# Two blocks on one core: where additions stand in VectorE's order, and what GpSimd adds for norms and gating

## The chip, the cores and the metric

The kernel runs on one core of one Trainium2 chip. The metric is the device time of one execution in microseconds (us), as the median of three runs. A core has a matrix engine (TensorE, PE in profile rows, with its weight loads as PEld), VectorE (DVE), ScalarE (ACT), GpSimd (POOL) and SyncE (SP). Each engine works through a queue of its own in order and waits on semaphores for what other engines or DMAs have to finish first. TensorE writes to PSUM; GpSimd works on SBUF.

## The reference, cut to what matters

One sequence of 512 tokens of width 1024 goes through a first block of two layers and a second block of two. All arithmetic is float32. What the change touches:

```python
def rms_norm(x, g):                       # before every mixer and every feed-forward half: 8 times
    y = x * rsqrt(mean(x * x, axis=-1) + EPS);  return y * g

def moe_swiglu(x, ...):                   # first block, second layer: 8 experts, 2 per token
    logits = x @ w_router + b_router;  top_logit, top_e = top_k(logits, 2);  top_w = softmax(top_logit)
    for e in range(8):                    # rows of the tokens that chose e
        h = silu(xb @ w_gate[e]) * (xb @ w_up[e]);  y[tokens] += (h @ w_down[e]) * w
    return y

def spatial_gating(u, v, v_g, w_s, b_s):  # second block, both layers: 4 heads of 64 channels
    v = rms_norm(v) * v_g
    # per head h, within each window of 128 tokens, with w_s masked to a causal pattern of blocks:
    # out[t, h, :] = u[t, h, :] * (sum over s in the window of w_s[h, t, s] * v[s, h, :]  +  b_s[h, t])
```

## The kernel before, in words

**Data.** The running activation lies transposed in eight tiles `s.xT[k]` of 128 channels x 512 tokens. Weights stream from DRAM in tiles of 128x1024 (`load`, L130). Each is split into a high half, a rounding to the matrix engine's faster float format by ScalarE (`hi`, L97), and a low half, the rest, by VectorE (`lo`, L113) or GpSimd (L111). A product then takes three matmuls: high x high, high x low, low x high (L138 to L140, in the experts L1067 to L1069). A raw tile has 8 buffers in the layer with the experts, the halves 5; so the splitting runs a few tiles ahead of TensorE and no more.

**Order.** A planner sets each engine's queue before the program runs. It goes by the order in the source, by modelled durations and by what it takes to be ready, and lets an instruction of lower rank run early where it takes its inputs to be there. `after(s, ins)` (L629) fixes one thing: what stands in its block is queued behind `ins` on that engine.

**Norms.** `norm_tile(k)` (L209) splits tile k and squares it (L219 ScalarE, L221 GpSimd). GpSimd adds squares 1 to 5 to square 0 in `sqa` (L225); squares 6 and 7 stay apart. `norm_end` (L227) sums the three tiles over channels with matmuls against a constant (L233), in the order `sqa`, 6, 7: four matmuls of 128x2 per tile, which the trace shows as eight records.

**Experts** (`moe`, L975). Behind the router eight 128x512 tiles of normalized tokens are made by transposes (L1044, in PSUM tags `sc` and `tp`, two banks each) and split. A branch (L1160) covers the case of overfull experts, which is not taken with these inputs. Experts 0 and 1 get their rows by a matmul with a one-hot matrix (L1170); the others gather theirs from `xn`, a copy in DRAM. For this copy GpSimd adds the high and low halves of the eight tiles (L1195) and stores them (L1196); its queue also holds the scatters into a small table (L1188) and the loads of it (L1199, L1201). Each expert is `up` (24 weight tiles in three column groups c of 8) and `down` (11 tiles f); a second group of tokens, 32 per expert, is multiplied from the raw tiles in float32 on a quarter of the columns (`others`, L1077). In experts 0 and 7 all low halves are VectorE's (`les` is "v").

Experts 0 to 6 scatter results to `ys` in DRAM. Expert 7 keeps its own in SBUF (`keep`), and meanwhile the rows of `ys` are loaded into pairs of tiles, `early`, by 16 loads on GpSimd's queue (L1252). `mid`, called behind each down tile f, adds each pair at f = 2 (L1300) and at f = 6 transposes the sums back (`sums`, L1144, one PSUM bank `st`) and adds them to `xT` (L254). A last stage multiplies expert 7's kept rows by one-hot matrices (L1314), adds them to `xT` and starts the next norm.

**Gating** (`gmlp`, L1722). For each of four heads: four float32 matmuls, one per 128 tokens, into PSUM partitions 0 to 63 (L1744, two records each), one more that adds the bias as a product with a row of ones (L1745), and a VectorE multiplication with 64 rows of `u` (L1748). The bias row is loaded into a rotating tile by ScalarE's queue (L1718). The result is split and used by `out_proj` at the layer's end. The state-space branch, run beside it, has a matmul group (L1626) that alternates between PSUM partitions 0 to 63 and 64 to 127.

Of the kernel before, what the change touches and what calls it, by code (L numbers as in the profile page):

```python
# [46 lines left out]
class Ctx:  # L47
# [58 lines left out]
    def lo(s, out, x, h, scale=None, eng="v"):  # L106
        nc = s.nc
        if scale is not None:
            nc.vector.scalar_tensor_tensor(out, x, scale, h.bitcast(F32), ALU.mult, ALU.subtract)  # L109
        elif eng == "p":  # L110
            nc.gpsimd.tensor_sub(out, x, h.bitcast(F32))  # L111
        else:
            nc.vector.tensor_sub(out, x, h.bitcast(F32))  # L113

    def split(s, x, h, l, scale=None, he="a", le="v"):
        s.hi(h, x, scale, he)
# [92 lines left out]
    def norm_tile(s, k):  # L209
        nc = s.nc  # L210
        g = s.gain[:, k:k + 1]
        h = s.xp.tile([128, S], F32R, name="xh", tag="xh")
        l = s.xp.tile([128, S], F32R, name="xl", tag="xl")
        s.split(s.xT[k], h, l, scale=g)
        s.xh.append(h)
        s.xl.append(l)
        t = s.sqa if k == 0 else s.sqtile()
        if k in s.SQ_ACT:
            nc.scalar.activation(t, s.xT[k], AF.Square)  # L219
        else:  # L220
            nc.gpsimd.tensor_mul(t, s.xT[k], s.xT[k])  # L221
        if k == 0 or k >= KT - 2:
            s.sqs = [t] if k == 0 else s.sqs + [t]
        else:
            nc.gpsimd.tensor_add(s.sqa, s.sqa, t)  # L225
# [749 lines left out]
def moe(s):  # L975
# [63 lines left out]
    xt = [None] * (2 * NT)  # L1039
    for hf in range(2):  # L1040
        for i in range(NT):
            ps = s.P(("sc", "tp")[i % 2])
            for k in range(4):
                nc.tensor.transpose(ps[:, k * 128:k * 128 + 128], s.xT[4 * hf + k][:, i * 128:i * 128 + 128], s.ident)  # L1044
            h = s.xp.tile([128, 512], F32R, name="xth", tag="xh")
            l = s.xp.tile([128, 512], F32R, name="xtl", tag="xl")
            s.hi(h, ps, s.rt[:, i:i + 1])
            with after(s, chosen):
                s.lo(l, ps, h, s.rt[:, i:i + 1])
            xt[2 * i + hf] = (h, l)  # L1050
# [12 lines left out]
    def load3(src, le):  # L1063
        return (*s.load(src, le=le), s.raw)
# [12 lines left out]
                    last = nc.tensor.matmul(out(j), lhs(k), rhs(raw, j), start=k == 0, stop=k == K - 1)  # L1077
        held.clear()

    def up(gu, X, first=(), les=MO_UP):  # L1080

        H, HO = [], s.A((128, FE * 32), F32)
        hold = 2 if s.more is None else HOLD
        for c, (f0, nb) in enumerate(FBLK):
            n = nb * 128
            pp, po, held = [s.P("mm"), s.P("sc")], s.P("o"), []
            for k in range(KT):
                i = KT * c + k
                wh, wl, raw = first.pop(0) if first else load3(gu(i)[:, :2 * n], les[i % len(les)])
                for x in range(2):  # L1090
                    o = slice(x * n, x * n + n)
                    mm3m(pp[x][:, :n], X[1 + k // 2][:, k % 2 * 256:k % 2 * 256 + 128], X[1 + k // 2][:, k % 2 * 256 + 128:k % 2 * 256 + 256],
                         wh[:, o], wl[:, o], k == 0, k == KT - 1)
                held.append((k, raw[:, :2 * n].rearrange("p (x j c) -> p x j c", x=2, j=nb)))
                if len(held) == hold or k == KT - 1:
                    others(held, nb, KT, lambda k: X[0][:, (CAP - 128) * k:(CAP - 128) * (k + 1)], lambda r, j: r[:, :, j],
                           lambda j: po[32 * j:32 * j + 32, 0:256].rearrange("p (x c) -> p x c", x=2))
            g, h = s.T(), s.T()
            nc.scalar.activation(g[:, :n], pp[0][:, :n], AF.Silu)
            nc.vector.tensor_mul(h[:, :n], pp[1][:, :n], g[:, :n])  # L1100
            r = slice(0, 32 * nb)
            go, ho = s.T((128, 128)), s.T((128, 128))
            nc.scalar.activation(go[r], po[r, 0:128], AF.Silu)
            nc.vector.tensor_mul(ho[r], po[r, 128:256], go[r])
            hh, hl = s.A(), s.A()
            with s.late(L_TP):
                ps = s.P("tp")
                for j in range(nb):
                    nc.tensor.transpose(ps[:, j * 128:j * 128 + 128], h[:, j * 128:j * 128 + 128], s.ident)
                s.split(ps[:, :n], hh[:, :n], hl[:, :n])  # L1110
                ps = s.P("tp")
                nc.tensor.transpose(ps[:, r], ho[r], s.ident[r, r])
                nc.scalar.activation(HO[:, 32 * f0:32 * f0 + 32 * nb], ps[:, r], AF.Copy)
            H.append((hh, hl))
        return H, HO

# [71 lines left out]
            nc.gpsimd.indirect_dma_start(out=s.tab[:, :], out_offset=bass.IndirectOffsetOnAxis(ap=place[:, k, i:i + 1], axis=0),  # L1188
                                         in_=m["info"][:, k, i], in_offset=None)

    for hf in range(2):
        for i in range(NT):
            h, l = xt[2 * i + hf]
            t = s.A((128, 512), F32)
            nc.gpsimd.tensor_add(t, h.bitcast(F32), l.bitcast(F32))  # L1195
            nc.gpsimd.dma_start(s.xn[hf * S + i * 128:hf * S + i * 128 + 128, :], t)  # L1196
    at = lambda r: bass.AP(tensor=s.tab.tensor, offset=s.tab.offset + 4 * r, ap=[[4, 32 if r else 128], [4 * CAP, NE], [1, 4]])
    kM, kO = (s.small((128, NE, 4), tag="k" + n, bufs=1) for n in "MO")
    nc.gpsimd.dma_start(kM, at(0))  # L1199
# [56 lines left out]
    for e in range(NE):  # L1256
        if e % 2 and e + 1 < NE:
            G = gather(e + 1)
        H = up(lambda i, e=e: a["moe_gu"][e * KT * len(FBLK) + i], X[e % 2], ahead, "v" if e in (0, NE - 1) else MO_UP)

        def put(x, ps, e=e):
            yt = s.T()
# [32 lines left out]
        s.split(ps, *(v[:, :n] for v in Y[x]), scale=wt[:, NE - 1, w:w + 1])  # L1295

    def mid(f):
        if f == 2:
            for y in chain(*early):
                nc.vector.tensor_add(y[0], y[0], y[1])  # L1300
        if f != 6:
            return
        for k, ps in sums(lambda hf, i: early[hf][i][0], "st"):
            s.residual(k, ps)
# [402 lines left out]
def gmlp_tables(s, L):  # L1707

    nc, a, mixp = s.nc, s.a, s.mixp
    vg = mixp.tile([128, 256], F32, name="vgain")  # L1710
    src = a["gmlp_vg"]
    nc.scalar.dma_start(vg, bass.AP(tensor=src.tensor, offset=src.offset + L * 256, ap=[[0, 128], [1, 256]]))
    wm = s.ldm("c_wmask", (128, 128))
    w = s.A((128, 4, 128), F32)
    nc.scalar.dma_start(w, a["gmlp_wT"][L])
    nc.gpsimd.tensor_mul(w, w, wm.unsqueeze(1).to_broadcast([128, 4, 128]))
    bs = s.T((1, 4, 128))
    nc.scalar.dma_start(bs, a["gmlp_bs"][L:L + 1])  # L1718
    return vg, w, bs


def gmlp(s, L, tabs, vps, u):  # L1722
# [15 lines left out]
        nc.vector.scalar_tensor_tensor(vn.rearrange("p h d -> p (h d)"), vps[c], y[:, c:c + 1], vg, ALU.mult, ALU.mult)  # L1738
        V.append(vn)
    yield 4  # L1740
    for h in range(4):
        ps = s.P(TG["gm"])
        for n in range(NT):
            nc.tensor.matmul(ps[0:64, n * 128:n * 128 + 128], V[n][:, h], w[:, h], start=n == 0, stop=False)  # L1744
        nc.tensor.matmul(ps[0:64], s.ones1[:, 0:64], bs[:, h:h + 1, :].to_broadcast([1, 4, 128]), start=False, stop=True)  # L1745
        t = u[h // 2]
        r = slice(64 * (h % 2), 64 * (h % 2) + 64)
        nc.vector.tensor_mul(t[r], ps[0:64], t[r])  # L1748
        if h % 2 == 1:
            s.dbg("d_sgu%d_%d" % (L, h // 2), t)  # L1750
            mix_tile(s, 2 + h // 2, t)
    yield 4


# [546 lines left out]
```

## Time and profile before

| | |
|---|---|
| median of 3 runs | 2829.59 us (2823.96 to 2833.44) |
| the profiled execution's own time | 2834.34 us |
| its span, first to last instruction | 2832.6 us |
| mean granted TensorE clock | 0.969 of full |
| busy: PE, DVE, ACT, POOL | 96%, 60%, 43%, 25% of the span |
| instructions | 39198 |
| moved by DMA | 354.42 MB, mean 125 GB/s |

The busy share of TensorE counts matmuls that overlap with the next one, so 96% is the share of the span in which at least one is under way. A row of a timeline has the start in us, the duration in us, the engine, the source line, the operation with the names of the tiles written and read, and, in brackets, the time for which the engine stood idle before it and what ended that. Neighbours of the same kind are merged (x8), with one start and one duration for all. In a list of waits the numbers are the total, the count and the longest.

### The profile page before, as it was taken

The page shows a single profiled execution, that of the slowest core. Times are in us where ns is not written, and L with a number is a line of the kernel's source. Part 1 is how long each engine was busy: PE and PEld are TensorE (multiplying, and loading weights), DVE is VectorE, ACT ScalarE, POOL GpSimd, SP SyncE. Part 2 cuts the span into 40 slices and gives each one's busy share as a digit, 9 for nine tenths or more (in the row PEclk, how much of TensorE's full clock was granted, in tenths as well). Part 3 has the DMA queues.
Part 4 walks back from the last instruction along what each step waited for, and adds up shares of the span by engine and source line. Part 5 has one row for each costly group of instructions (what it writes and reads, how often), then busy time and mean ns, then how long its engine had stood idle before and what let it go on. Part 6 is the DMA issues. An engine that isn't in the chain of part 4 may idle for free.

```text
span 2832.6 us, 39198 instructions
## 1 busy us (share of the span) xinstructions
PE 2722.8 (96%) x14791; PEld 2149.2 (76%) x14791; DVE 1708.1 (60%) x3125; ACT 1209.3 (43%) x1969; POOL 696.3 (25%) x549
## 2 busy tenths in 40 slices
PE   8989999999999899999998999999999998999999
PEld 6767778888888767676765786778888886788887
DVE  3666759556444466655565647676475456775573
ACT  3545654222322356665564424444243234443342
POOL 3300014223312143333332231032023130122120
PEclk8979999999999899999999998999999998999999
DMA  3200113334342167776777641132323320222322
GB/s 132 92 28 19 42 64 121 105 119 158 127 141 82 37 221 270 264 271 247 271 258 286 174 118 41 39 112 89 105 97 104 122 75 15 82 96 88 106 93 91
DMA packets 122008, 354.42 MB, mean 125 GB/s; under 512 B 17106, under 2 KB 28690, under 8 KB 121300
## 3 DMA queue, kind: packets, MB, share of 16 engines
q1 hardware_dynamic: 106208, 316.40, 33.2%
q0 software_dynamic: 10272, 31.29, 3.2%
q10 hardware_dynamic: 5332, 4.15, 0.5%
q8 instruction: 118, 1.93, 0.3%
q14 instruction: 78, 0.64, 0.1%
HBM read 330.66 MB, written 21.15 MB: 124 GB/s over the span
## 4 chain that ended last, share of the span: by engine, by line
PE 57%; DMA 3%; DVE 2%; ACT 1%; issue 1%; POOL 1%; SPq 0%; ACTq 0%; POOLq 0%; DVEq 0%
PE psmm L138 5%; PE psmm L139 5%; PE psmm L140 5%; PE pso L1077 4%; PE pstp L140 3%; PE pstp L139 3%; PE pstp L138 3%; PE pssc L140 3%; PE pssc L139 3%; PE pssc L138 3%; PE psmm L1068 2%; PE psmm L1067 2%; PE psmm L1069 2%; PE pssc L1068 2%; PE pssc L1069 2%; PE pssc L1067 2%
## 5 line engine op out<-in xcount | busy, mean ns | idle before, releaser
L97 ACT ACTIVATE whi<-raw 128x1024 fp32r<-128x1024 f32 (+5 forms) x663 | 626.4, 947 | 971.1 <-PE psmm L139 328.6
L113 DVE TENSOR_TENSOR wlo<-raw,whi 128x1024 fp32r<-128x1024 f32 (+3 forms) x596 | 717.7, 1210 | 410.7 <-ACT whi L97 392.9
L138 PE MATMUL psmm<-xh,whi 128*128 128x512 f32 x688 | 275.5, 401 | 12.5 <-ACT xh L99 11.0
L139 PE MATMUL psmm<-xl,whi 128*128 128x512 f32 x688 | 273.1, 397 | 2.7 <-DVE xl L109 2.5
L140 PE MATMUL psmm<-xh,wlo 128*128 128x512 f32 x688 | 273.2, 397 | 0.1
L111 POOL TENSOR_TENSOR wlo<-raw,whi 128x1024 fp32r<-128x1024 f32 (+3 forms) x67 | 142.1, 2121 | 337.6 <-ACT whi L97 296.2
L139 PE MATMUL pssc<-xl,whi 128*128 128x512 f32 x448 | 175.1, 391 | 0.0
L140 PE MATMUL pssc<-xh,wlo 128*128 128x512 f32 x448 | 174.9, 390 | 0.0
L138 PE MATMUL pssc<-xh,whi 128*128 128x512 f32 x448 | 174.7, 390 | 0.0
L138 PEld LDWEIGHTS psmm<-xh,whi 128*128 128x128 f32 x688 | 130.9, 191 | 43.1 <-ACT xh L99 11.8
L2008 POOL TENSOR_TENSOR T<-T 128x512 f32<-128x512 f32 x44 | 57.1, 1297 | 416.0 <-DVE T L2005 353.1
L139 PE MATMUL pstp<-xl,whi 128*128 128x512 f32 x400 | 156.1, 390 | 0.0
L138 PE MATMUL pstp<-xh,whi 128*128 128x512 f32 x400 | 155.8, 390 | 0.0
L140 PE MATMUL pstp<-xh,wlo 128*128 128x512 f32 x400 | 155.8, 389 | 0.0
L139 PEld LDWEIGHTS psmm<-xl,whi 128*128 128x128 f32 x688 | 131.1, 191 | 32.0 <-DVE xl L109 5.0
L140 PEld LDWEIGHTS psmm<-xh,wlo 128*128 128x128 f32 x688 | 131.1, 191 | 28.8 <-DVE wlo L113 1.0
L1077 PE MATMUL pso<-raw,A 128*32 128x256 f32 x2112 | 151.5, 384 | 0.0
L111 POOL TENSOR_TENSOR A<-T,A 128x512 fp32r<-128x512 f32 (+1 forms) x78 | 125.9, 1614 | 102.9 <-ACT A L97 102.8
L1068 PE MATMUL psmm<-wlo,A 128*128 128x512 f32 (+1 forms) x280 | 115.4, 412 | 22.3 <-DVE wlo L113 18.5
L1077 PEld LDWEIGHTS pso<-raw,A 128*32 128x32 f32 x2112 | 65.3, 109 | 69.2 <-issue 32.2
L254 DVE TENSOR_TENSOR xT<-psmm,xT 128x512 f32<-128x512 f32 x90 | 61.8, 688 | 89.1 <-PE psmm L140 88.6
L1067 PE MATMUL psmm<-whi,A 128*128 128x512 f32 (+1 forms) x280 | 114.0, 407 | 1.0 <-ACT whi L97 1.0
(665 smaller groups left out, 6106.4 us busy)
## 6 DMA issues: line engine op xcount, KB each, us to landing
raw<-moe_gu SPq DMA_DIRECT2D x128, 512.0 KB
raw<-moe_dn SPq DMA_DIRECT2D x88, 512.0 KB
raw<-w_up_t SPq DMA_DIRECT2D x88, 512.0 KB
raw<-moe_gu SPq DMA_DIRECT2D x64, 384.0 KB
raw<-ffn_gu SPq DMA_DIRECT2D x44, 512.0 KB
raw<-od_w_in_t SPq DMA_DIRECT2D x24, 512.0 KB
raw<-w_in_t SPq DMA_DIRECT2D x24, 512.0 KB
raw<-w_down_t SPq DMA_DIRECT2D x32, 384.0 KB
```

Of the source, the lines that this page charges most:

```text
L97: nc.scalar.activation(out, x, AF.Copy)
L111: nc.gpsimd.tensor_sub(out, x, h.bitcast(F32))
L113: nc.vector.tensor_sub(out, x, h.bitcast(F32))
L138: nc.tensor.matmul(ps, wh, xh, start=first, stop=False)
L139: nc.tensor.matmul(ps, wh, xl, start=False, stop=False)
L140: nc.tensor.matmul(ps, wl, xh, start=False, stop=last)
L254: s.nc.vector.tensor_add(s.xT[m], ps, s.xT[m])
L1067: nc.tensor.matmul(ps, xh, wh, start=first, stop=False)
L1068: nc.tensor.matmul(ps, xh, wl, start=False, stop=False)
L1069: nc.tensor.matmul(ps, xl, wh, start=False, stop=last)
L1077: last = nc.tensor.matmul(out(j), lhs(k), rhs(raw, j), start=k == 0, stop=k == K - 1)
L2008: nc.gpsimd.tensor_mul(acc[1], acc[1], acc[0])
```

## The change

- Norms: square 6 is added to `sqa` by GpSimd as well, so `norm_end` sums two tiles.
- The transposes ahead of the experts go round three PSUM tags in place of two.
- `lo` remembers VectorE's last subtraction in `s.low`. `up` takes a function `each`, called ahead of every weight tile. For expert 0 this is `row(i)`: ahead of tiles 3 to 10 it issues one addition for `xn`, on VectorE, behind the subtraction last issued, and its store on GpSimd's queue. The loop that did the eight additions on GpSimd is gone.
- In expert 7 the eight merging additions are issued four behind tile f = 4's subtraction and four behind that of f = 5; the transposes back at f = 7.
- Gating: the bias is loaded to all 128 partitions by two DMAs, into a tile of its own. Heads go in pairs: head 2x in PSUM partitions 0 to 63 and head 2x+1 in 64 to 127, their matmuls alternating in a fixed order. The bias matmul is gone; GpSimd multiplies `u` by the bias beforehand, VectorE multiplies PSUM by `u` for both heads at once, and GpSimd adds the two.

```diff
@@ -110,7 +110,7 @@
         elif eng == "p":
             nc.gpsimd.tensor_sub(out, x, h.bitcast(F32))
         else:
-            nc.vector.tensor_sub(out, x, h.bitcast(F32))
+            s.low = nc.vector.tensor_sub(out, x, h.bitcast(F32))
 
     def split(s, x, h, l, scale=None, he="a", le="v"):
         s.hi(h, x, scale, he)
@@ -219,7 +219,7 @@
             nc.scalar.activation(t, s.xT[k], AF.Square)
         else:
             nc.gpsimd.tensor_mul(t, s.xT[k], s.xT[k])
-        if k == 0 or k >= KT - 2:
+        if k == 0 or k == KT - 1:
             s.sqs = [t] if k == 0 else s.sqs + [t]
         else:
             nc.gpsimd.tensor_add(s.sqa, s.sqa, t)
@@ -1039,7 +1039,7 @@
     xt = [None] * (2 * NT)
     for hf in range(2):
         for i in range(NT):
-            ps = s.P(("sc", "tp")[i % 2])
+            ps = s.P(("sc", "tp", "mm")[(NT * hf + i) % 3])
             for k in range(4):
                 nc.tensor.transpose(ps[:, k * 128:k * 128 + 128], s.xT[4 * hf + k][:, i * 128:i * 128 + 128], s.ident)
             h = s.xp.tile([128, 512], F32R, name="xth", tag="xh")
@@ -1077,7 +1077,7 @@
                     last = nc.tensor.matmul(out(j), lhs(k), rhs(raw, j), start=k == 0, stop=k == K - 1)
         held.clear()
 
-    def up(gu, X, first=(), les=MO_UP):
+    def up(gu, X, first=(), les=MO_UP, each=None):
 
         H, HO = [], s.A((128, FE * 32), F32)
         hold = 2 if s.more is None else HOLD
@@ -1086,6 +1086,8 @@
             pp, po, held = [s.P("mm"), s.P("sc")], s.P("o"), []
             for k in range(KT):
                 i = KT * c + k
+                if each is not None:
+                    each(i)
                 wh, wl, raw = first.pop(0) if first else load3(gu(i)[:, :2 * n], les[i % len(les)])
                 for x in range(2):
                     o = slice(x * n, x * n + n)
@@ -1188,12 +1190,16 @@
             nc.gpsimd.indirect_dma_start(out=s.tab[:, :], out_offset=bass.IndirectOffsetOnAxis(ap=place[:, k, i:i + 1], axis=0),
                                          in_=m["info"][:, k, i], in_offset=None)
 
-    for hf in range(2):
-        for i in range(NT):
-            h, l = xt[2 * i + hf]
-            t = s.A((128, 512), F32)
-            nc.gpsimd.tensor_add(t, h.bitcast(F32), l.bitcast(F32))
-            nc.gpsimd.dma_start(s.xn[hf * S + i * 128:hf * S + i * 128 + 128, :], t)
+    def row(i):
+        hf, i = divmod(i - 3, NT)
+        if not 0 <= hf < 2:
+            return
+        h, l = xt[2 * i + hf]
+        t = s.A((128, 512), F32)
+        with after(s, s.low):
+            nc.vector.tensor_add(t, h.bitcast(F32), l.bitcast(F32))
+        nc.gpsimd.dma_start(s.xn[hf * S + i * 128:hf * S + i * 128 + 128, :], t)
+
     at = lambda r: bass.AP(tensor=s.tab.tensor, offset=s.tab.offset + 4 * r, ap=[[4, 32 if r else 128], [4 * CAP, NE], [1, 4]])
     kM, kO = (s.small((128, NE, 4), tag="k" + n, bufs=1) for n in "MO")
     nc.gpsimd.dma_start(kM, at(0))
@@ -1256,7 +1262,7 @@
     for e in range(NE):
         if e % 2 and e + 1 < NE:
             G = gather(e + 1)
-        H = up(lambda i, e=e: a["moe_gu"][e * KT * len(FBLK) + i], X[e % 2], ahead, "v" if e in (0, NE - 1) else MO_UP)
+        H = up(lambda i, e=e: a["moe_gu"][e * KT * len(FBLK) + i], X[e % 2], ahead, "v" if e in (0, NE - 1) else MO_UP, row if e == 0 else None)
 
         def put(x, ps, e=e):
             yt = s.T()
@@ -1295,10 +1301,11 @@
         s.split(ps, *(v[:, :n] for v in Y[x]), scale=wt[:, NE - 1, w:w + 1])
 
     def mid(f):
-        if f == 2:
-            for y in chain(*early):
-                nc.vector.tensor_add(y[0], y[0], y[1])
-        if f != 6:
+        if f in (4, 5):
+            with after(s, s.low):
+                for y in early[f - 4]:
+                    nc.vector.tensor_add(y[0], y[0], y[1])
+        if f != 7:
             return
         for k, ps in sums(lambda hf, i: early[hf][i][0], "st"):
             s.residual(k, ps)
@@ -1714,8 +1721,10 @@
     w = s.A((128, 4, 128), F32)
     nc.scalar.dma_start(w, a["gmlp_wT"][L])
     nc.gpsimd.tensor_mul(w, w, wm.unsqueeze(1).to_broadcast([128, 4, 128]))
-    bs = s.T((1, 4, 128))
-    nc.scalar.dma_start(bs, a["gmlp_bs"][L:L + 1])
+    bs = mixp.tile([128, 2, 128], F32, name="gbias")
+    src = a["gmlp_bs"]
+    for c in range(2):
+        nc.scalar.dma_start(bs[64 * c:64 * c + 64], bass.AP(tensor=src.tensor, offset=src.offset + L * 512 + c * 128, ap=[[0, 64], [256, 2], [1, 128]]))
     return vg, w, bs
 
 
@@ -1738,17 +1747,18 @@
         nc.vector.scalar_tensor_tensor(vn.rearrange("p h d -> p (h d)"), vps[c], y[:, c:c + 1], vg, ALU.mult, ALU.mult)
         V.append(vn)
     yield 4
-    for h in range(4):
-        ps = s.P(TG["gm"])
+
+    for x in range(2):
+        ps, t, ub, last = s.P(TG["gm"]), u[x], s.T((128, 4, 128)), None
+        nc.gpsimd.tensor_mul(ub, t.rearrange("p (n q) -> p n q", n=4), bs[:, x].unsqueeze(1).to_broadcast([128, 4, 128]))
         for n in range(NT):
-            nc.tensor.matmul(ps[0:64, n * 128:n * 128 + 128], V[n][:, h], w[:, h], start=n == 0, stop=False)
-        nc.tensor.matmul(ps[0:64], s.ones1[:, 0:64], bs[:, h:h + 1, :].to_broadcast([1, 4, 128]), start=False, stop=True)
-        t = u[h // 2]
-        r = slice(64 * (h % 2), 64 * (h % 2) + 64)
-        nc.vector.tensor_mul(t[r], ps[0:64], t[r])
-        if h % 2 == 1:
-            s.dbg("d_sgu%d_%d" % (L, h // 2), t)
-            mix_tile(s, 2 + h // 2, t)
+            for c in range(2):
+                with after(s, last):
+                    last = nc.tensor.matmul(ps[64 * c:64 * c + 64, n * 128:n * 128 + 128], V[n][:, 2 * x + c], w[:, 2 * x + c], start=True, stop=True)
+        nc.vector.tensor_mul(t, ps, t)
+        nc.gpsimd.tensor_add(t, t, ub.rearrange("p n q -> p (n q)"))
+        s.dbg("d_sgu%d_%d" % (L, x), t)
+        mix_tile(s, 2 + x, t)
     yield 4
```

## Rows read from the trace of the kernel before

**Rows 1.** The page: busy time by engine; GB/s in 40 equal slices.

```profile
PE 2722.8 (96%) x14791; PEld 2149.2 (76%) x14791; DVE 1708.1 (60%) x3125; ACT 1209.3 (43%) x1969; POOL 696.3 (25%) x549
...
GB/s 132 92 28 19 42 64 121 105 119 158 127 141 82 37 221 270 264 271 247 271 258 286 174 118 41 39 112 89 105 97 104 122 75 15 82 96 88 106 93 91
```

**Rows 2.** Waits of TensorE, whole span: us in total, times, longest.

```profile
PE psmm L1068 <- DVE wlo L113: 18.5, 7, 11.0
```

**Rows 3.** Timeline, expert 0: start, duration, engine, line, operation [idle before <-releaser].

```profile
998.66 9.88 POOL L1195 TENSOR_TENSOR A<-xth,xtl 128x512 f32<-128x512 f32 x8
...
1000.82 11.09 DVE L113 TENSOR_TENSOR wlo<-raw,whi 128x1024 fp32r<-128x1024 f32 x3 [0.78 <-ACT whi L97]
...
1009.69 0.80 PE L1068 MATMUL psmm<-wlo,A 128*128 128x512 f32 x1 [5.82 <-DVE wlo L113]
```

**Rows 4.** Windows: length; busy PE, PEld, DVE, ACT, POOL; clock; DMA share; GB/s.

```profile
1009.60:1015.00 5.40, 5.31 (x13) 4.18 (x14) 3.52 (x4) 1.70 (x2) 5.07 (x9) 0.54 0.81 208
...
1519.00:1531.00 12.00, 1.03 (x10) 0.41 (x3) 2.80 (x4) 1.06 (x1) 7.33 (x14) 0.67 0.93 332
...
1530.70:1537.00 6.30, 6.23 (x20) 3.63 (x20) 6.30 (x9) 1.01 (x2) 3.05 (x6) 0.52 0.84 318
...
1637.70:1651.00 13.30, 13.28 (x79) 8.91 (x80) 4.73 (x8) 0.00 (x0) 0.00 (x0) 1.00 0.10 39
```

**Rows 5.** Timeline at expert 7: GpSimd, VectorE, TensorE.

```profile
1522.02 4.86 POOL L1252 DMA_DIRECT2D A<-ys  x9 [8.64 <-issue]
...
1527.18 0.69 DVE L1300 TENSOR_TENSOR A<-A 128x512 f32<-128x512 f32 x1 [12.71 <-DMA A<-ys]
...
1530.77 0.80 PE L1068 MATMUL psmm<-wlo,A 128*128 128x512 f32 x1 [10.97 <-DVE wlo L113]
```

**Rows 6.** VectorE groups, 1010:1030 (first row), 1555:1584: busy, mean ns, idle before.

```profile
L113 DVE TENSOR_TENSOR wlo<-raw,whi 128x1024 fp32r<-128x1024 f32 x11 | 13.4, 1222 | 5.6 <-ACT whi L97 5.5
...
L113 DVE TENSOR_TENSOR wlo<-raw,whi 128x1024 fp32r<-128x1024 f32 x13 | 15.5, 1218 | 4.3 <-ACT whi L97 4.2
...
L254 DVE TENSOR_TENSOR xT<-psst,xT 128x512 f32<-128x512 f32 x5 | 3.4, 688 | 4.4 <-PE psst L1144 4.4
```

**Rows 7.** DMA issues: tile, queue, count, KB each, median us to landing.

```profile
A<-ys POOLq DMA_DIRECT2D x16, 256.0 KB, 4.9
```

**Rows 8.** Timeline of the norms' sums on TensorE (two norms).

```profile
778.87 0.95 PE L233 MATMUL psst<-inv_d,sqa 128*128 128x2 f32 x8
...
779.68 1.03 PE L233 MATMUL psst<-inv_d,T 128*128 128x2 f32 x8
...
2465.87 1.05 PE L233 MATMUL psst<-inv_d,sqa 128*128 128x2 f32 x8 [0.73 <-POOL sqa L225]
```

**Rows 9.** Line L225: ns min/median/max, first and last start.

```profile
L225 POOL TENSOR_TENSOR sqa<-sqa,T x35: 1291/1608/2272, 394.6 to 2464.2; 128x512 f32<-128x512 f32 x35
```

**Rows 10.** Timeline of TensorE in gating and state-space part, layer 0.

```profile
1646.45 1.09 PE L1744 MATMUL pstp<-A 128*64 128x128 f32 x8
...
1647.47 1.07 PE L1745 MATMUL pstp<-T,ones 1*64 1x512 f32 x2
...
1648.47 1.09 PE L1744 MATMUL pstp<-A 128*64 128x128 f32 x8
...
1652.70 2.08 PE L1626 MATMUL pstp<-s5U,A 128*64 128x64 f32 x64
```

**Rows 11.** Timeline at the experts' end: ScalarE, TensorE.

```profile
1591.88 0.72 ACT L99 ACTIVATE xh<-xT,pack_all 128x512 fp32r<-128x512 f32 x1 [5.53 <-DMA s5C<-dC]
...
1592.65 0.73 PE L138 MATMUL psmm<-xh,whi 128*128 128x512 f32 x2 [1.57 <-ACT xh L99]
```

**Rows 12.** Timeline of TensorE at the first dispatch matmul of expert 0.

```profile
985.78 0.61 PE L1170 MATMUL psst<-A,xth 128*128 128x320 f32 x1 [5.25 <-DVEq L1160]
```

**Rows 13.** Timeline of VectorE at a norm behind a mixing layer.

```profile
1848.34 1.78 DVE L109 SCALAR_TENSOR_TENSOR xl<-xT,pack_all,xh 128x512 fp32r<-128x512 f32 x1
...
1853.48 0.73 DVE L109 SCALAR_TENSOR_TENSOR xl<-xT,pack_all,xh 128x512 fp32r<-128x512 f32 x1
```

## The prediction

> **What bounds the kernel now.** I read the page first: TensorE is busy 96% of the span [rows 1], every other engine 60% or less, so time is won in two ways only: TensorE gets less to do, or one of its waits goes. The page says nothing of where the other 4% lie, so the second view is TensorE's waits. Its largest line is a matmul of the experts (L1068) that waits for VectorE's low half of a weight tile: 18.5 us, one wait alone 11.0 [rows 2]. Third, the timelines around the two long waits, because a wait names the last releaser and not what held it up; and the windows for the clock that follows. Last, the stretches in which the changed lines run.
>
> The first long wait is in expert 0. GpSimd runs eight additions back to back, 998.66 to 1008.54. VectorE's subtraction for a weight tile starts at 1000.82, and three of them take 11.09 us [rows 3] where one takes 1.22 [rows 6]. TensorE has other matmuls until about 1003.9, then stands 5.82 us [rows 3]. It comes back slow: the granted clock is 0.54 in the 5.4 us behind the wait, about the lower of its two levels (1.2 of 2.4 GHz) [rows 4].
>
> The second is in expert 7. VectorE's first addition of the merging (L1300) waits 12.71 us for rows of `ys` from DRAM [rows 5]; the weight subtractions are queued behind it on VectorE, and TensorE stands 10.97 us and returns at 0.52 for 6.3 us [rows 4, 5]. The source has this addition in the down half of the expert, the queue order has it in the up half: the planner believed the data to be there.
>
> **The change, part by part.** The sum is made against the profiled execution's own 2834.3 us (span 2832.6, 1.7 around it); the median of the three runs, 2829.6, is 4.7 below that, and what is saved is taken off it unchanged.
>
> A. *Expert 0: eight additions leave GpSimd and are tied, one by one, behind the subtractions of weight tiles 2 to 9 on VectorE.* Gone is the wait, 5.82, and the slow stretch: 5.31 us busy at 0.54 would be 2.9 at full clock, so 2.4. Together 8.2. The additions read tiles that have long been written, so they wait for nothing. Price on VectorE: one 128x512 addition took 0.69 [rows 5], eight about 5.5, between subtractions; in 1010 to 1030 VectorE had 5.6 us of idle time before its subtractions [rows 6]. The cover is all used up, and one late subtraction is what TensorE sees next. I charge 1.7 (bounds 0, all hidden, and 5.5, none). GpSimd's queue gets the eight stores to `xn` after the small table scatters and loads rather than between them; by the source the first reader of `xn` is the gather for expert 2, after expert 0. Net **6.5** (2.7 to 8.2).
>
> B. *Expert 7: the eight merging additions are tied behind the low half of down tiles 4 and 5, the merging transposes move from tile 6 to tile 7.* The down tiles' subtractions run in 1555 to 1584 [rows 6], 28 us and more behind the stall's place, so the data is there. Gone: 10.97, and 6.23 us at 0.52, so 3.0: 14.0. What is late next: (1) the DMAs. In the stall the weight stream pauses while 16 reads of 256 KB [rows 7] run; without it both run together. 332 GB/s at a share of 0.93 [rows 4] is some 357 in all; the expert slices move about 261 on average [rows 1], which leaves 96. The 4.2 MB need 44 us at that rate. Tile 4 comes some 7 us into that stretch, at about 1562, and 14 earlier after the change: 26 us behind the first read at 1522 [rows 5]. That is 1.7 MB too much, 6.5 us of weight stream. Converted tiles lie ready ahead of TensorE and absorb part; I charge 4 (0 to 6.5). (2) VectorE in the down half, 1555 to 1584, has 4.3 us idle before its subtractions [rows 6], 4.4 more before the merging's residuals that already run there [rows 6], and gets eight additions more, 5.5: charge 1 (0 to 4). The eight merging sums share one PSUM bank, so each waits for VectorE; from tile 7 on they run into the last stage, which needs them one by one. Net **9** (3.5 to 14).
>
> C. *Norms: the seventh square tile is added by GpSimd, not summed by TensorE.* Each of 8 norms loses 8 matmul records: one eight starts at 778.87 and the next at 779.68, so eight take 0.81 [rows 8]. 8 x 0.81 = 6.5. In the two mixing layers TensorE also stands 0.73 for `sqa` (one of the two: [rows 8]) at a place in its queue where it comes before the seventh square is there; with the longer sum the planner must put these matmuls later, so 1.4 more. Against it, one GpSimd addition more per norm, 1.61 [rows 9], which is hidden where the tiles come far apart (behind the feed-forward halves), and for which I charge 0.6 in each of the three norms with tiles close together, the two behind the mixing layers and the one behind the experts (0 to 1.6). Net **6** (3.1 to 7.9).
>
> D. *Gating: the bias leaves TensorE, and two heads share a PSUM tile.* Per layer four bias groups of 1.00 go (1647.47 to 1648.47): 4.0. The heads' 32 records take 1.02 per eight (1646.45 to 1647.47), 4.1 in all [rows 10]. In the new order they alternate between PSUM's lower and upper 64 partitions, as the state-space matmuls do: 64 records with half the columns in 2.08, so 32 of full width in about 2.1 [rows 10]: 2.0 saved. TensorE is full here (13.28 of 13.30 us [rows 4]), so 6.0 per layer comes through, 12 for two. From below: if pairs don't overlap, 8. The new GpSimd multiplications and additions (1.24 each by expert 0's [rows 3] to 1.61 by the norms' [rows 9]) feed tiles that by the source only out_proj reads, at the layer's end, and behind the addition that waits for VectorE GpSimd has only the state-space branch's next step; VectorE's four multiplications become two. I take 0.5 off for what falls due elsewhere. Net **11.5** (7.5 to 12).
>
> E. *Two bias loads on ScalarE's queue in place of one.* The old one needed a tile of the rotating pool, the new ones have their own and are free to issue at the experts' end, where ScalarE is already held up 5.53 us by loads in its queue and TensorE stands 1.57 for it [rows 11]. Bounds: 0, and one such hold, 5.5. I take **1.5** lost.
>
> The third PSUM bank for the transposes ahead of expert 0 I put at nothing: what follows, the first dispatch matmul, waits 5.25 for VectorE's arrival at the branch [rows 12], which the additional bank does not hasten; if it did, under 1 us.
>
> Sum: 6.5 + 9 + 6 + 11.5 - 1.5 = 31.5. 2834.3 - 31.5 = 2802.8 for a profiled run, 2829.6 - 31.5 = **2798** for the median.
>
> **The rivals.**
> 1. *The waits change their name.* TensorE still stands in both experts: for weights in expert 7 (6.5 and the clock behind it, 1.5), for VectorE in expert 0 (5.5), plus the late sums (4). A and B then bring 2.7 and 2 rather than 6.5 and 9: 20.7 us in all, 2809. For it: the DMAs are at 0.93 while `ys` is read [rows 4]. Against: the reads have 26 us and weight tiles lie ready. It decides in expert 7, from the point where a weight tile lands later than TensorE asks.
> 2. *GpSimd takes what it gives.* Expert 0 shows that GpSimd's additions stop VectorE's two-input work whole. The norm windows show it smaller: a VectorE instruction of 0.73 takes 1.78 while GpSimd adds [rows 13]. The change puts 8 additions in norms and 8 instructions in gatings on GpSimd, 16 x 1.61 = 25.8 us. If two thirds came back as VectorE delay that TensorE sees, 17 of the 31.5 are gone: 2815. Against: TensorE is the late one there, and VectorE 60% busy [rows 1]. The Trainium skill (SBUF — State Buffer, section "SBUF: two separate sides") states that the two engines share a port pair by an exclusive lock for the full instruction, so the loser blocks and doesn't merely slow down. By that rule each addition would hold VectorE for its whole 1.61; the trace of expert 0 agrees (11.09 us for three), the 1.78 shows a hold of about 1.05.
> 3. *Slower: a new queue order with new stalls.* The planner orders all queues from modelled durations, and the change alters durations in every norm. One instruction that waits for a DMA at the head of VectorE's or ScalarE's queue costs what the one in expert 7 did, 14 us. Two take 28 and leave the kernel about where it was; from three on it is slower, 2829.6 - 31.5 + 42 = 2840. For it: the trace has one such stall of full size that the planner did not foresee [rows 5]. Against: one in 2.8 ms, and the two known ones are now bound to a place.
> 4. *All gross terms come through*: 8.2 + 14 + 7.9 + 12 = 42, 2787.
>
> **How the numbers follow.** Forecast (within 9 us of 2798) 0.55, rival 1 0.18, rival 2 0.10, all gross 0.10, rival 3 0.07. The last splits into 0.04 slower and 0.03 about even. The range goes from the gross case less 3 to beyond rival 2: 2784 to 2820. A change of 0.3% is 8.5 us, about what a measurement of this kernel tells from none, so faster means below 2821: 0.55 + 0.18 + 0.10 + 0.10, less 0.03 for tails: 0.90. Within 0.3%: 0.06. Slower: 0.04.
>
> **What would show it.** A: no wait of L1068 over 1 us at expert 0, and subtractions of 1.2 us there. B: the merging additions in the down half with no wait for `ys`; a wait of L1068 for `whi` or a raw tile instead would be rival 1. C: 16 in place of 24 matmul records per norm and no wait for `sqa`. D: no bias matmuls, 16 head records in about 1.05 us; 2.0 would mean that pairs don't overlap. E: ScalarE's wait ahead of the norm at the experts' end longer than 8 us in all. The prediction is wrong if TensorE's busy time falls by less than 14 us, or if a wait of over 8 us stands somewhere new.

## The result and the profile after

The changed kernel takes 2798.2 us (median of 4 runs, 2792.1 to 2801.2), the kernel before 2826.8 beside it: ratio 0.9893, 95% interval 0.9873 to 0.9914, some 30 us less. The profiled spans differ by 33.2 (2832.6 to 2799.4).

The page's busy times and TensorE's waits (total, times, longest), answering to [rows 1, 2]:

```profile
PE 2692.2 (96%) x14711; PEld 2126.4 (76%) x14711; DVE 1710.0 (61%) x3129; ACT 1213.9 (43%) x1972; POOL 700.9 (25%) x557
```

```profile
PE psmm L138 <- ACT xh L99: 14.7, 2, 8.2
PE psst L1172 <- DVEq L1162: 8.0, 1, 8.0
...
PE psmm L1068 <- DVE wlo L113: 4.7, 7, 2.0
```

L1068's wait fell from 18.5 to 4.7. What is new lies in the first line: one of its two waits, 8.2, is at the span's start and was there before; the other, 6.5, is in the experts' last stage. The second line is the wait at the branch, 5.25 before [rows 12].

Where the time went is read from when TensorE starts the same instruction in each trace. Below, the start in the kernel before, and how much earlier (-) the others start it. Executions differ by themselves: row, merge and gate change nothing ahead of expert 0 and begin it 3.4 apart, and row makes a step of 2.3 between the gatings, where it changes nothing. The traced execution of the kernel before took 2834.3, some 7.6 above its median here, and all ten begin expert 0 earlier than it, so the foot of a column overstates a gain: row ends 8.6 earlier and is no faster. So only the step from one line to the next is read, and a step of 2 is nothing.

```text
                      before   after    row  merge   norm   gate  sums6 2banks  t_late untied  combo
expert 0, first        996.2    -3.0   -1.8   -5.2   -3.9   -1.8   -7.6   -7.3   -3.5   -5.4   -5.1
expert 0, down part   1076.5    -9.6   -4.8   -6.3   -6.4   -3.1  -14.4  -16.1  -12.2   -4.1  -13.5
expert 7, up part     1515.5    -7.3   -5.5   -7.9   -6.2   -4.5  -15.1  -15.1  -10.4   -0.5  -15.9
last stage, first     1584.3   -21.8   -5.3  -23.0   -7.0   -5.1  -29.7  -30.0  -25.1   -2.3  -31.4
behind last stage     1606.2   -14.9   -5.9  -11.8   -6.4   -5.6  -23.3  -22.3  -18.8   +0.9  -25.4
behind gating 1       1675.2   -24.0   -5.9  -12.2   -7.8  -11.4  -32.3  -31.4  -27.9   -8.3  -27.8
ahead of gating 2     2227.4   -26.8   -8.2  -11.8   -9.9  -12.0  -35.5  -34.0  -33.5  -15.0  -31.2
behind gating 2       2289.1   -33.1   -8.2  -11.8   -6.9  -18.2  -41.7  -40.3  -39.8  -21.2  -37.5
last matmul           2827.6   -33.2   -8.6  -12.0   -9.3  -19.2  -44.8  -45.8  -46.6  -27.8  -43.1
```

Timelines of the changed kernel, VectorE and TensorE at expert 0, answering to [rows 3]:

```profile
997.77 1.89 DVE L1200 TENSOR_TENSOR A<-xth,xtl 128x512 f32<-128x512 f32 x3
999.57 1.22 DVE L113 TENSOR_TENSOR wlo<-raw,whi 128x1024 fp32r<-128x1024 f32 x1
...
1021.00 0.18 DVE L1211 CAST rows<-kM 128x8 int32<-128x8 f32 x1 [4.60 <-DMA kM<-tab]
...
1025.32 0.51 PE L1068 MATMUL psmm<-wlo,A 128*128 128x512 f32 x1 [1.97 <-DVE wlo L113]
```

The subtraction is back at 1.22 and the 5.82 us wait is gone. But VectorE now stands three times (4.60, 1.23, 0.95) for small tables that come by DMA (L1211 to L1219), with weight tiles queued behind; TensorE waits 1.97 and 0.79 for those.

Expert 7 (VectorE) and the last stage: ScalarE's and SyncE's queues, TensorE, and the windows of the clock behind the wait and of the transfers ahead of it (columns as in [rows 4]):

```profile
1549.43 2.49 DVE L1307 TENSOR_TENSOR A<-A 128x512 f32<-128x512 f32 x4
```

```profile
1559.91 6.99 SPq L1620 DMA_DIRECT2D s5T<-dK  x8
...
1570.80 1.37 SPq L130 DMA_DIRECT2D raw<-w_in_vg  x2
...
1567.69 0.33 ACTq L1722 DMA_DIRECT2D A<-gmlp_wT  x1
1572.91 0.33 ACTq L1719 DMA_DIRECT2D vgain<-gmlp_vg  x1
...
1574.97 0.72 ACT L99 ACTIVATE xh<-xT,pack_all 128x512 fp32r<-128x512 f32 x1 [11.52 <-DMA A<-gmlp_wT]
...
1575.74 1.22 PE L138 MATMUL psmm<-xh,whi 128*128 128x512 f32 x2 [6.52 <-ACT xh L99]
```

```profile
1564.00:1570.00 6.00, 5.11 (x23) 3.39 (x23) 3.96 (x7) 0.00 (x0) 1.04 (x1) 1.00 1.16 161
...
1575.74:1581.00 5.26, 5.26 (x15) 4.25 (x16) 4.25 (x6) 2.16 (x4) 3.33 (x3) 0.55 1.01 356
```

The merging additions run without a wait, 14.5 us are won up to the last stage, and 6.9 of them are lost in it: ScalarE's splits of `xT` stand behind loads in its own queue, and TensorE comes back at a clock of 0.55. In 1564 to 1570 the DMA engines are full and move only 161 GB/s.

The 6.9 are not all waiting. These are the windows of the last stage in the kernel before and in the changed one:

```profile
1584.34:1606.17 21.83, 17.25 (x73) 12.56 (x69) 14.76 (x20) 8.38 (x14) 11.34 (x9) 1.00 1.06 226
...
1562.56:1591.25 28.69, 21.23 (x90) 16.42 (x89) 18.32 (x26) 8.94 (x14) 13.04 (x10) 0.88 0.77 178
```

TensorE idles 2.9 longer (4.6 before, 7.5 after) and works 4.0 longer: 20 of the 32 transposes of the merging sums, all of them ahead of this stage in the kernel before, now stand in it, and part of it runs at the slow clock.

SyncE's loads also stand in another order. In the kernel before, the first tile of `w_in_vg`, weights of the next projection, goes out 4.4 us ahead of the last stage's first matmul (1584.34), and the last five of the eight loads of `s5T` 9 to 15 us behind it:

```profile
1579.96 0.35 SPq L130 DMA_DIRECT2D raw<-w_in_vg  x1
...
1587.15 12.91 SPq L1613 DMA_DIRECT2D s5T<-dK  x6
```

In the changed kernel `w_in_vg` goes out 8.2 us behind that matmul (1562.56), and seven of the eight loads of `s5T` are out by 1563.2. Every trace with the tied merging has this order (t_pool apart); row, norm, gate and untied have the weights first and `s5T` spread out.

Norms and gating on TensorE, answering to [rows 8, 10]: 16 records per norm in place of 24, no wait for `sqa`, and 16 records of two heads in the time of 8.

```profile
2440.37 0.95 PE L233 MATMUL psst<-inv_d,sqa 128*128 128x2 f32 x8
2441.18 1.03 PE L233 MATMUL psst<-inv_d,T 128*128 128x2 f32 x8
...
1620.02 1.09 PE L1757 MATMUL pstp<-A 128*64 128x128 f32 x16 [1.17 <-DVE A L1747]
```

### The profile page after: what moved, and what is told of

Read it like the earlier page. It is cut to its first block, busy times and chain, and to the rows that moved or that the text cites. A ratio compares the mean times of both kernels' runs of the same rounds, so it can differ in the third digit from the quotient of the medians.

```text
span 2799.4 us, 39072 instructions
## 1 busy us (share of the span) xinstructions
PE 2692.2 (96%) x14711; PEld 2126.4 (76%) x14711; DVE 1710.0 (61%) x3129; ACT 1213.9 (43%) x1972; POOL 700.9 (25%) x557
## 4 chain that ended last, share of the span: by engine, by line
PE 56%; DMA 3%; DVE 3%; issue 1%; ACT 1%; POOL 1%; SPq 0%; ACTq 0%; POOLq 0%; DVEq 0%
PE psmm L138 5%; PE psmm L139 5%; PE psmm L140 5%; PE pso L1077 4%; PE pstp L138 3%; PE pstp L140 3%; PE pstp L139 3%; PE pssc L138 3%; PE pssc L140 3%; PE pssc L139 3%; PE psmm L1068 2%; PE psmm L1067 2%; PE psmm L1069 2%; PE pssc L1069 2%; PE pssc L1068 2%; PE pssc L1067 2%
## 5 line engine op out<-in xcount | busy, mean ns | idle before, releaser
L138 PEld LDWEIGHTS psmm<-xh,whi 128*128 128x128 f32 x688 | 131.2, 191 | 49.3 <-ACT xh L99 15.1
L1068 PE MATMUL psmm<-wlo,A 128*128 128x512 f32 (+1 forms) x280 | 114.7, 410 | 9.9 <-POOL wlo L111 5.3
```

Of the source, the lines that this page charges most:

```text
L138: nc.tensor.matmul(ps, wh, xh, start=first, stop=False)
L1068: nc.tensor.matmul(ps, xh, wl, start=False, stop=False)
```

## The experiments

All ratios are to the kernel before, in the same comparison.

**Each part alone**, on the kernel before: the hunks of `lo`, `up`, `row` (row_only); of `lo`, `mid` (merge_only); of `norm_tile` (norm_only); of `gmlp_tables`, `gmlp` (gate_only), for instance

```diff
-        if k == 0 or k >= KT - 2:
+        if k == 0 or k == KT - 1:
```

> The kernel before with the change to expert 0 alone (eight additions on VectorE, each behind a weight tile's subtraction). Theory (the gain is local and its price is a later load of the tables): TensorE's waits for VectorE at expert 0 fall from 5.8 us to about 2.8, the slow-clock stretch goes, 6.5 us less up to expert 1 and in all. Rival (the gain is given back in experts 1 to 7, where the change's trace loses another 2.3): 4 us less in all. In both, nothing changes before expert 0.

Measured 1.0007 (0.9995 to 1.0019), no gain. The long wait goes, 7.9 us are won by 1014, and 4.9 come back: VectorE stands 9.3 us (7.40, 0.76, 1.18) for the tables, TensorE 4.35.

```profile
1025.69 0.17 DVE L1211 CAST rows<-kM 128x8 int32<-128x8 f32 x1 [7.40 <-DMA kM<-tab]
...
1030.01 0.80 PE L1068 MATMUL psmm<-wlo,A 128*128 128x512 f32 x1 [4.35 <-DVE wlo L113]
```

The price is where the theory has it but larger (4.35 for 2.8), and the net of 6.5 is refuted, as is the rival's 4: 3.0 in the trace, none in the time.

> The kernel before with the change to expert 7's merging alone. Theory (the merging sums, moved to tile 7, run into the last stage and delay it): 14 us less up to the last stage, some 7 given back there, 7 less in all. Rival (what is given back there comes from the two bias loads on ScalarE's queue, which this kernel does not have): 14 us less in all, TensorE's waits in the last stage as before, 1.6 and 1.3.

0.9996 (0.9986 to 1.0005). 15.1 us are won up to the last stage and 11.2 lost in it, without the two new bias loads: the rival falls. The theory's net of 7 falls too, the time gains 1.1 (from 1.4 lost to 4.0 won).

```profile
1578.80 0.72 ACT L99 ACTIVATE xh<-xT,pack_all 128x512 fp32r<-128x512 f32 x1 [16.61 <-DMA A<-gmlp_wT]
...
1579.58 1.22 PE L138 MATMUL psmm<-xh,whi 128*128 128x512 f32 x2 [11.60 <-ACT xh L99]
```

> The kernel before with the seventh square's addition on GpSimd alone. Theory (eight matmul records less per norm, 0.8 each, and two waits of 0.7 gone, some given back to GpSimd's later sum): 5 to 6 us less. Rival (the other queue order in the first layer, which wins 2.9 in the change's trace between its two norms, comes with it): 8 to 9 less. Second rival (what is saved in a norm comes back as a wait for the sum): 0 to 2 less.

0.9967 (0.9955 to 0.9979), 9.3 us (5.9 to 12.7). Expert 0 begins 3.9 earlier, within the 1.8 to 5.2 of the three versions that change nothing ahead of it, so no gain of the first layer beyond its norms is seen, and the first rival's reason has no support though its size fits; the interval just holds the theory's 6.

> The kernel before with the change to the gating alone, bias loads included. Theory (6.3 less per gating, the loads cost under 2): 11 to 12.5 us less. Rival (the two loads hold ScalarE at the experts' end and give back the 7 us that the change's trace loses there): 5 to 6 less, with TensorE's wait for ScalarE in the last stage at 6 rather than 1.6.

0.9953 (0.9937 to 0.9970), 13.3 us (8.5 to 17.8); by the table the gatings win 5.8 and 6.2. In the last stage nothing is lost (-5.1, -5.6) and TensorE waits 1.34 and 1.70 for ScalarE, as in [rows 11]: the two bias loads cost nothing.

**What holds the last stage**, on the changed kernel.

```diff
-        if f != 7:
+        if f != 6:
```

> The changed kernel with the merging sums back at down tile 6. Theory one (the late sums delay the last stage): the 7 us that the last stage gives back come in, 7 less than the changed kernel, 0.9868 of the kernel before. Theory two (the last stage waits because ScalarE's first loads for the gating stand behind the eight loads of s5T, whatever the sums do): within 2 of the changed kernel, TensorE's wait for ScalarE's xh at 5 to 9 us there.

0.9886 (0.9861 to 0.9910); TensorE's wait there is 6.29. These are theory two's numbers, but the edit does not test theory one: the planner left the sums where they were. The first of the eight stands 13.0 us ahead of the last stage's first matmul in place of 11.9, the other seven as in the changed kernel, from 1.8 ahead to 26.5 behind (26.9 there). The second and the last, in sums_6 (first matmul at 1554.63) and in the changed kernel:

```profile
1552.79 0.60 PE L1146 MATMUL psst<-pack_all,A 128*128 128x128 f32 x4
...
1581.11 0.60 PE L1146 MATMUL psst<-pack_all,A 128*128 128x128 f32 x4
```

```profile
1560.71 0.60 PE L1146 MATMUL psst<-pack_all,A 128*128 128x128 f32 x4
...
1589.43 0.60 PE L1146 MATMUL psst<-pack_all,A 128*128 128x128 f32 x4
```

```diff
-    nc.scalar.dma_start(w, a["gmlp_wT"][L])
+    nc.sync.dma_start(w, a["gmlp_wT"][L])
...
```

> The changed kernel with the gating's loads (gmlp_vg, gmlp_wT, gmlp_bs) issued by SyncE, not ScalarE. Theory two (a load at the head of ScalarE's queue holds the splits behind it): TensorE's wait of 6.5 us in the last stage is gone or under 2, 5 to 7 us less than the changed kernel. Theory one (late sums): no change there. Third outcome (the loads now hold up SyncE's weight stream): the wait turns into one for raw tiles in the projections behind, 0 to 3 less.

0.9895 (0.9871 to 0.9919); the wait stays, 6.63. It decides nothing: loads of other small tables (`c_wmask` first) were left on ScalarE's queue and the first of them waited as long.

```diff
-        nc.sync.dma_start(T[16 * j:16 * j + 16].rearrange...
+        nc.gpsimd.dma_start(T[16 * j:16 * j + 16].rearrange...
```

> The changed kernel with the eight loads of s5T issued by GpSimd, not SyncE. Theory (ScalarE's loads for the gating wait for earlier transfers of the hardware queues, the s5T loads among them, and hold the splits behind): ScalarE's idle time of 11.5 us in the last stage falls below 6, TensorE's wait there from 6.5 to under 2, 5 to 6 us less than the changed kernel. Rival (what ScalarE waits for is the memory that the first block gives back, late whatever is loaded): the wait stays at 5 or more, no gain.

0.9887 (0.9867 to 0.9907). The theory's numbers fail; the rival's come true, but not its reason: `vgain`, the load that needs memory given back, is out at 1559.25, early. ScalarE stands as long as before, now for a load behind other transfers, and TensorE 6.57 and 2.64:

```profile
1553.34 4.47 POOL L1620 DMA_DIRECT2D s5T<-dK  x8 [13.80 <-PE pssc L1069]
...
1568.76 0.72 ACT L99 ACTIVATE xh<-xT,pack_all 128x512 fp32r<-128x512 f32 x1 [11.58 <-DMA raw<-w_in_vg]
```

So it is not these eight loads at that place in SyncE's queue. Here the two loads of `w_in_vg` go out at 1553.69, ahead of the stage as in the kernel before, while `s5T` is loaded at once beside them, and 10.5 us are lost in the stage: the weights' place alone does not bring it back.

**The places.**

```diff
-        with after(s, s.low):
+        with after(s, None):
```

> The changed kernel without the two ties: the additions for xn and for the merging stand where the planner puts them on VectorE. Theory (the given place, not the engine or the place in the source, takes the stall of expert 7 away): additions stand in the up half again and wait for the rows of ys, TensorE stands 8 to 14 us there, 6 to 10 us more than the changed kernel in all, since part of it is won back in the last stage. In expert 0 the additions are free of waits wherever they stand: no change. Rival (the place in the source, tiles 4 and 5, is enough): no change in either.

0.9936 (0.9916 to 0.9955), some 12 us more than the changed kernel. The stall of expert 7 is back in full, TensorE waits 11.04:

```profile
1526.35 0.69 DVE L1307 TENSOR_TENSOR A<-A 128x512 f32<-128x512 f32 x1 [12.90 <-DMA A<-ys]
```

The expectation for expert 0 was wrong: five additions run ahead of the first weight tile and expert 0 loses 1.3 rather than winning 6.6 (waits 2.22 for a raw tile, 2.06 for VectorE). VectorE itself stands 9.43 there for a high half, so what is late is the weight tile, not an addition; why it is late was not tested. The engine alone is not enough in either place.

```diff
+        if i == 18:
+            with after(s, s.low):
+                tables()        # the reading of kM and kO, L1211 to L1224
```

> The changed kernel with VectorE's reading of the small tables (rows, gat, wt, ltok) tied behind the subtraction of weight tile 17 of expert 0. Theory (in the changed kernel they wait 6.8 us for tables at the head of VectorE's queue and TensorE waits 2.8 for the weight tiles behind them): those two waits go, 2 to 3 us less by the end of expert 0, and the last three additions for xn come 10 us earlier. Rival (VectorE is the late one there whatever stands in its queue): the waits stay under the name of ScalarE's high halves, 0 to 1 less.

0.9870 (0.9851 to 0.9890). VectorE reads the tables at 1025.99 without a wait, the last additions run at 1018.19, and no wait of TensorE is left at expert 0. Its gain there is 8.7 in place of 6.6, but two_banks, where the tables are read as before, has 8.8: the waits go, their worth in time is not shown.

```diff
-        for n in range(NT):
-            for c in range(2):
+        for c in range(2):
+            for n in range(NT):
```

> The changed kernel with each head of a pair finished before the other begins (same matmuls, same PSUM tile, order alone). Theory (two heads overlap because they alternate between the lower and the upper 64 columns of the engine): 16 records take 2.0 us in place of about 1.05, 2 us more per gating, 4 more in all. Rival (the overlap does not depend on the order): no change.

0.9874 (0.9849 to 0.9899), not told apart from the changed kernel in time. In the trace:

```profile
1611.16 1.09 PE L1757 MATMUL pstp<-A 128*64 128x128 f32 x8 [1.18 <-DVE A L1747]
...
1614.39 2.24 PE L1757 MATMUL pstp<-A 128*64 128x128 f32 x24
```

Eight alone take 1.09, as before, but 24 take 2.24, not 3.3: only heads of one pair were kept apart, and the next pair's first head may run beside the second of this one (argued, not shown). So 32 records take 3.3 in place of 2.2: the order matters, at half the expected size.

```diff
-            ps = s.P(("sc", "tp", "mm")[(NT * hf + i) % 3])
+            ps = s.P(("sc", "tp")[i % 2])
```

> The changed kernel with the transposes ahead of the experts on two PSUM banks again. Theory (behind the transposes TensorE waits for VectorE at the branch, so an earlier end only lengthens that wait): within 1 us of the changed kernel, the branch wait near 5 in place of 8. Rival (the third bank is worth what the transposes gain): 1.5 to 3 more.

0.9870 (0.9843 to 0.9897), not told apart from the changed kernel, the branch wait 5.6 in place of 8.0. The third bank brings nothing that shows.

**Together.** Two banks, the tables late, and the small loads of the second block on GpSimd:

```diff
+    s.ldq = nc.gpsimd
...
-    nc.scalar.dma_start(w, a["gmlp_wT"][L])
+    s.ldq.dma_start(w, a["gmlp_wT"][L])
```

> The changed kernel with three edits: two PSUM banks for the transposes again, VectorE's reading of the small tables behind weight tile 17 of expert 0, and all loads of the second block's small tables on GpSimd's queue, so that ScalarE issues none. Theory (a load in ScalarE's queue waits for earlier transfers, whichever these are, and the splits wait behind it): ScalarE's idle time in the last stage falls from 11.5 us to under 3 and TensorE's wait there from 6.5 to under 1.5, worth 6; expert 0 keeps 9 rather than 6.5; in all 2786 to 2790, 0.986 of the kernel before. Rival (the transfers themselves are the limit there, and the weights behind them come as late): the wait of 5 to 6 us stays in the last stage or just behind it, under the name of a raw tile or of GpSimd's later squares, 2791 to 2795.

0.9889 (0.9866 to 0.9912). ScalarE's own loads no longer hold it: the first splits run at 1557.53, as soon as `xT` is there. Then it stands for a weight tile that is behind the state-space tables, TensorE waits 4.78 and, at 1602, 4.33 for VectorE:

```profile
1557.53 1.34 ACT L99 ACTIVATE xh<-xT,pack_all 128x512 fp32r<-128x512 f32 x2 [3.65 <-DVE xT L254]
...
1571.87 1.06 ACT L97 ACTIVATE whi<-raw 128x1024 fp32r<-128x1024 f32 x1 [8.94 <-DMA raw<-w_in_vg]
...
1573.59 1.22 PE L138 MATMUL psmm<-xh,whi 128*128 128x512 f32 x2 [4.78 <-ACT xh L99]
```

```profile
1549.00:1572.00 23.00, 18.87 (x90) 14.32 (x89) 14.21 (x20) 6.80 (x12) 12.66 (x15) 1.00 1.03 225
```

The rival holds: the transfers fill the DMA engines for 23 us, and whoever needs the last of them waits. The sums stand as late here, so the first splits also show that it was not the sums that held them. Untied apart, no version is told apart from the changed kernel: the intervals of tables_late and two_banks (0.9870) overlap with its own. Loading `s5T` behind the projection's weights, which its first use at 1636 would allow, was not tried.

## Why the prediction was right, point by point

The sum came out (31.5 against 30 by the ratio, 33.2 in the spans), in part by luck: A and B came near their figures because about what was charged against each was lost, but elsewhere and for another reason, while C, D and E brought more than was put down for them.

- A, 6.5: 6.6 up to expert 0's down part (4.3 to 7.4 in sums_6, tables_sp, t_pool and no_alt, which have the same code there). The charge of 1.7 for a VectorE without cover was the wrong step: the additions fit in. They do not stand one by one either: five run by 1003.5, the last three at 1026.97, behind the tables. The price was 2.8, tables read at the head of VectorE's queue, so A's sign, no wait over 1 us, failed (1.97); alone (row_only) it took nearly all. This is the mechanism of rival 3, an instruction that waits for a DMA ahead of weight tiles, at a fifth of the size given. The Trainium skill (SBUF — State Buffer, section "SBUF: two separate sides") has a GpSimd instruction that reads SBUF and a VectorE one with two inputs there lock each other out; the subtraction's 1.22 us with the additions gone agrees.
- B, 9: 14.5 - 6.9 = 7.6. The gross term came out, though 2 to 3 of the 14.5 are the transposes that only moved into the last stage. Step (1) failed: no weight tile of expert 7 was late for the reads of `ys` (waits of 0.2). The loss came in the last stage, where the prediction had only late sums, inside a charge of 1. Three things change there together: the stall no longer gives the second block's tables and weights time, SyncE's loads stand in another order, and the sums run late. What holds ScalarE is its own loads and the transfers behind them; which of the first two makes these late no run separates. Rival 1 had the kind right, a stall that turns into a wait for transfers, but not the place; a new order of loads is rival 3's kind.
- C, 6: 9.3 alone (5.9 to 12.7). Perhaps sized a little low; both waits for `sqa` are gone, as predicted.
- D, 11.5: 12.6, 6.3 from the first head of each gating to behind it, as sized: the pairs overlap.
- E, -1.5: nothing. Its sign, a wait of ScalarE over 8 us, did appear (11.52), but from B's change: merge_only has 16.61 without the new loads, and gate_only, which has them, loses nothing. By the prediction's last line this is also a new wait of over 8, if ScalarE's count; TensorE's part of it is 6.52. The third bank, nothing, as said.
- Rival 2 did not come: norms and gating, which give GpSimd the work, bring 9.3 and 13.3 alone, no less than was added up for them, and VectorE's busy time is 1710.0 after, 1708.1 before.

That the parts don't add looks likely and is not shown: alone they win 21.7 (-2.0, 1.1, 9.3, 13.3), together 30, with intervals of some 3 to 5 on each and 6 on the whole, which taken together leave some 9 either way (an estimate). A and B bring nothing measurable alone; in company some 8 are left for them when C and D are taken off at what they bring alone. The 12 of untied are something else: the price of taking the ties out of the changed kernel, whose additions then still are VectorE's; its expert 0 loses 1.3 even against the kernel before. In the traces less comes back in company: TensorE waits 4.35 behind the tables alone and 2.8 together, and the last stage loses 11.2 alone and 6.0 to 7.7 together (10.5 in t_pool). The 2.3 lost in experts 1 to 6 are within what executions differ by. Why the tables land earlier in company was not tested.

## What to carry to other kernels

Where a planner orders queues from modelled times, tie to a place what waits for a DMA, and look at once for what else of that kind stands at the head of the same queue: here taking two stalls of 17 us away exposed two others of 9 us. A stall also gives the transfers time; ask which burst comes next and whether it fits without that time. A part tried alone can show nothing because what it wins is lost again some us later: merge_only won 15.1 and lost 11.2. And where a planner orders the queues, read from the trace whether an edit moved what it was meant to move; in sums_6 it did not.

## What was not expected of the hardware

DMA engines that are full need not be fast. `s5T` comes in eight loads of 128 KB in pieces of 512 bytes, 9.7 us each to land. The window of 1564 to 1570 still has the end of `s5C` in it, in larger pieces; in 1566 to 1570 there are pieces of 512 bytes and a few smaller ones alone, the engines' share is 1.21, and they move 124 GB/s. In 1574 to 1577, with pieces of 2 and 4 KB, they move 393 at a share of 1.04. These are the packets of the two windows in the changed kernel:

```profile
DMA packets 1027, 0.50 MB, mean 124 GB/s; under 512 B 58, under 2 KB 1027, under 8 KB 1027
...
DMA packets 496, 1.18 MB, mean 393 GB/s; under 512 B 53, under 2 KB 69, under 8 KB 496
```

The Trainium skill (DMA: Bandwidth & Descriptors, the table at its head) gives 512 bytes as enough for line rate; these pieces, of that size, reached about a third of the rate of the larger ones, so here the measurement decides. Whether the size does it, or that each load goes to 16 partitions only, was not tested.
